# A delta-rule inverse from blocks of 16, with rows spread over partitions through DRAM instead of by products

## The chip, the cores and the metric

The kernel runs on one core of a Trainium2 chip. The metric is the device time of one execution in microseconds, as the median of several runs. Before the change it is 1660.73 us (three runs, 1659.98 to 1662.09).

The core has five engines that matter here, each working through its own list of instructions in order and waiting on semaphores for the others: TensorE (matrix products; PE in the profile, with the load of its weights as PEld), VectorE (DVE), ScalarE (ACT), GpSimd (POOL) and SyncE (SP), which only issues DMAs. TensorE writes its products into PSUM; everything else lives in SBUF, which has 128 partitions.

## What is computed

The reference is one step of a decoder layer over 256 prompt tokens and 32 sample tokens (8 sequences of 4). Cut to what matters:

```python
proj = x @ w_in                                   # 2048 -> 11280 columns
y_a  = (gB * conv3(gC * h)) @ w_a_out             # short gated convolution
q, k, v = split(silu(conv4(qkv)))                 # then the gated delta rule, 8 heads of 128
gcum  = cumsum(g)  within chunks of 64
decay = exp(gcum_i - gcum_j)  for i >= j
M = strict_lower(kb @ k.T * decay)
T = inverse(I + M)                                # 64 x 64, unit lower triangular, per chunk and head
u = T @ (v * beta);  w = T @ (kb * exp(gcum))
# scan over the 4 chunks with a state S (128 x 128 per head), then norm and gate
y_b = o @ w_b_out
x = LN(ALPHA * x + (sig(m_a) * y_a + sig(m_b) * y_b) @ w_o)
x = LN(ALPHA * x + relu(x @ w_up)**2 @ w_down)
```

All of it is float32. The inverse T and the decay are what the change touches.

## The kernel before

**Weight blocks.** The bulk is x @ W for six weight matrices, cut into 496 blocks of 512 KB each. `load` (line 177) brings a block in on SP's queue into one of four buffers `raw`; `split_hi` (line 187) rounds it on ScalarE into a high half `hi`; `split_lo` (lines 189 to 194, seen at line 142 because all VectorE products, sums and differences go through the helper `tt`) subtracts to get the low half `lo`; `matmuls` (lines 219 and 221) multiplies: 24 products per block, high with high, high with low, low with high. High and low halves have four buffers each, and both splits are issued three blocks ahead of their use (`AHEAD`). A weight load can go out when the low half of the block four before it is made, since that frees the buffer.

**Steps.** The main loop (lines 1644 to 1735) issues one step per block. In each, in this order: the high half three blocks ahead; one portion of the side work, up to the next `yield` of a generator; the low half three blocks ahead; what is due of the evacuations of finished column groups; the block's 24 products; the weight load seven blocks ahead. The order is written by hand. Nothing is rescheduled, so the side work's instructions stand on each engine between those of the weight stream, at the step where their `yield` puts them.

**Evacuations.** Blocks 0 to 47 give k, q and v of the two groups of four heads. Each group of four blocks is followed by a convolution of four taps per half: copies on ScalarE, three VectorE instructions over 312 columns each (line 145), and then a SiLU on ScalarE (lines 291 to 298).

**Side work.** `side` runs `gates`, then `gdn(0)`, then `gdn(1)`, one for each group of four heads. `gates` (line 1017) computes g and its sums in chunks. `gdn` (line 1122) goes through the delta rule. Its parts around the change are:

- Decay: the elements of g are multiplied with a triangular mask into `gl` (128 x 512), split into two rounded halves `glx`, and multiplied with a matrix of ones per chunk (line 1214), which gives every partition the running sums along a row. From this the exponent `E` is made.
- `nM`, the negative of M, stands with a 64-row chunk on each half of the partitions; eight such matrices lie side by side.
- Inverse of the diagonal blocks of 8: they are gathered into `n8` (line 1269), spread into `X` (512 wide), split into two rounded halves `mx`, and multiplied with a matrix of ones per block of 8 (line 1333), so that each partition holds all rows of its own block. Seven forward-substitution steps on VectorE (lines 1339 and 1340) give the inverse `u8`, one product and one sum over the eight matrices at a time.
- Joining blocks: the loop over s = 8, 16 (line 1356) joins neighbouring blocks, with two sets of small 32 x 32 products in each round (`pairs`, line 1328), a copy on ScalarE, and a predicated copy and a transpose on VectorE. A last round joins 32 to 64.
- Then the state products, the scan over the chunks, and the sample tokens.

`gdn(1)` begins only when `gdn(0)` has ended, and all side work has to end before the block `mark["merge"]` = 112, where the pool of its tiles is given up.

Of the kernel before, what the change touches and what calls it, by code (L numbers as in the profile page):

```python
# [9 lines left out]
F32 = mybir.dt.float32  # L10
F32R = mybir.dt.float32r
# [29 lines left out]
def _constants():  # L41
# [7 lines left out]
    f["hm"] = k // 64 == m // 64  # L49
    i = np.arange(64)[None, :]  # L50
    f["lc"] = (k % 64) <= i
    f["mbias"] = np.where((k % 64) <= i, 0.0, -1e30)
    f["mask8"] = (k % 64) // 8 == i // 8
    f["m8"] = (k % 32) // 8 == i[:, 0:32] // 8
    f["i8"] = k % 8 == np.arange(8)[None, :]
    f["i8u"] = k % 8 < np.arange(8)[None, :]
    f["bo8"] = k // 8 == m // 8
# [20 lines left out]
    early = ("hm", "bo8", "lcum", "lrem", "lcums", "lrems", "lsp", "bm3", "hmask")  # L78
# [11 lines left out]
    for s in (8, 16):  # L90
        g[s] = (j // (2 * s) == i // (2 * s)) & ((j // s) % 2 == 0) & ((i // s) % 2 == 1)
# [14 lines left out]
def hybrid_kernel(ctx: ExitStack, tc: tile.TileContext, A):  # L106
# [3 lines left out]
    def pool(name, bufs=1, **kw):  # L110
        return ctx.enter_context(tc.tile_pool(name=name, bufs=bufs, **kw))
# [6 lines left out]
    gp = pool("gp", 4, space=PSUM)  # L118

# [21 lines left out]
    def tt(out, a, b, op):  # L141
        dve.tensor_tensor(out=out, in0=a, in1=b, op=op)  # L142
# [114 lines left out]
    hmr, bo8 = (cp.tile([P, P], F32R, name=n) for n in ("hmr", "bo8"))  # L257
# [759 lines left out]
    def gates(first):  # L1017
# [17 lines left out]
        for t, n in ((hmr, "hm"), (bo8, "bo8")):  # L1035
            act.copy(t, cst(n))
# [30 lines left out]
        tt(gm, bmid(g[:, 2, :], 8), bc(cst("bm3"), 8), MUL)  # L1067
        sb = cp.tile([P, 2, 8], F32, name="gsb")
# [13 lines left out]
        pe.matmul(q[:, 136:144], cst("lrems"), g[:, 2, :], start=True, stop=True)  # L1082
        ge = cp.tile([P, 96], F32, name="gexp")
# [38 lines left out]
    def gdn(G):  # L1122
# [26 lines left out]
        gl = T([P, 4, 2, 64], "gl")  # L1149
# [38 lines left out]
        for n in range(4):  # L1188
# [7 lines left out]
        tt(gl, bc(G_["g"][:, :, pr], 64),  # L1196
           cst("lc").unsqueeze(1).unsqueeze(1).to_broadcast([P, 4, 2, 64]), MUL)
# [3 lines left out]
        glf = gl.rearrange("p c r x -> p (c r x)")  # L1201
        glx = pl.tile([P, 2, 512], F32R, tag="vml", name=nm("glx"))
# [9 lines left out]
        gr = gtile()  # L1212
        for u in range(2):
            pe.matmul(gr, hmr, glx[:, u], start=(u == 0), stop=(u == 1))
# [12 lines left out]
        tt(E, gr.rearrange("p (c r x) -> p c r x", c=4, r=2), bc(G_["ngc"][:, :, pr], 64), ADD)  # L1227
# [35 lines left out]
        n8 = sqr[:, 0:64].rearrange("p (q j) -> p q j", q=8)  # L1263
        u8 = sqr[:, 64:128].rearrange("p (q j) -> p q j", q=8)
        t8 = sqr[:, 128:192].rearrange("p (q j) -> p q j", q=8)
        i8 = cst("i8")
        tt(Tm, nM, bmid(cst("mask8"), 8), MUL)
        yield
        dve.tensor_reduce(out=n8, in_=Tm.rearrange("p q (b j) -> p q j b", b=8), axis=mybir.AxisListType.X, op=ADD)
        tt(n8, n8, bmid(cst("i8u"), 8), MUL)  # L1270
        tt(n8, n8, bmid(i8, 8), ADD)
        tt(X.rearrange("p q (k j) -> p q k j", k=8), n8.unsqueeze(2).to_broadcast([P, 8, 8, 8]),
           i8.unsqueeze(1).unsqueeze(3).to_broadcast([P, 8, 8, 8]), MUL)
        move_sums(1)
        yield
        Xf = X.rearrange("p q c -> p (q c)")
        mx = pl.tile([P, 2, 512], F32R, tag="vml", name=nm("mx"))
        act.copy(mx[:, 0], Xf)
# [11 lines left out]
        tt(mx[:, 1], Xf, mx[:, 0], SUB)  # L1290
# [40 lines left out]
        n88 = gtile()  # L1331
        for u in range(2):
            pe.matmul(n88, bo8, mx[:, u], start=(u == 0), stop=(u == 1))
        nb = n88.rearrange("p (q k j) -> p q k j", q=8, k=8)
        dve.tensor_copy(u8, bmid(i8, 8))
        for j in range(1, 8):
            if j == 5 or j == 3 and G == 0:
                yield
            tt(t8[:, :, 0:j + 1], u8[:, :, 0:j + 1], nb[:, :, 0:j + 1, j], MUL)
            dve.tensor_reduce(out=u8[:, :, j], in_=t8[:, :, 0:j + 1], axis=mybir.AxisListType.X, op=ADD)  # L1340
        tt(U.rearrange("p q (b j) -> p q b j", b=4), u8.unsqueeze(2).to_broadcast([P, 8, 4, 8]),
           cst("m8").rearrange("p (b j) -> p b j", b=4).unsqueeze(1).to_broadcast([P, 8, 4, 8]), MUL)
# [13 lines left out]
        for s in (8, 16):  # L1356
            px = gtile()
            pairs(px, lambda r, q, w: nM[r, q, 32 * (w % 2):32 * (w % 2) + 32], Tc)
            act.copy(Xc, px[:, 0:256].rearrange("p (q c) -> p q c", q=8))
            if s == 16:  # L1360
                move_v(1)
            yield
            pq = gtile()
            pairs(pq, lambda r, q, w: Xc[r, q, :], U)
            dve.copy_predicated(U, bmid(msk(s), 8), pq[:, 0:256].rearrange("p (q c) -> p q c", q=8))
            dve.transpose(out=Tf, in_=Uf)
            if s == 16:
                states_of(0)
            move_v(0 if s == 8 else 2)
            yield  # L1370
# [398 lines left out]
```

## Time and profile before

| | before |
|---|---|
| median of three runs | 1660.73 us (1659.98 to 1662.09) |
| span of the profiled execution | 1656.8 us |
| the profiled execution's own time | not listed apart from its span |
| TensorE busy | 1648.6 us, 13130 products |
| VectorE busy | 981.2 us, 1299 instructions |
| ScalarE busy | 785.8 us, 1231 instructions |
| GpSimd busy | 138.8 us, 273 instructions |
| DMA | 280.42 MB, 169 GB/s on average |

The profile shows one execution. The span goes from its first to its last instruction. A timeline row gives the start from the span's begin, the time, the engine, the line of the kernel, the operation, the tile written and those read, the shape and the number of instructions merged; in brackets stands the idle time before it and what ended it. A product in float32 is issued as two instructions, so 32 products show as x64. Products overlap: the pitch between starts, not the length, is what one takes from TensorE. In the list of DMAs a row has the number, the size and the median time from issue to landing.

### The profile page before, as it was taken

How to read it: one execution, taken by the hardware profiler on the slowest of the kernel's cores; microseconds unless marked ns; L12 is line 12 of the kernel's file. 1: busy time of each engine (PE TensorE's matmuls, PEld its weight loads, DVE VectorE, ACT ScalarE, POOL GpSimd, SP SyncE). 2: the span in 40 equal slices, each digit the busy share in tenths (PEclk: the TensorE clock that was granted, in tenths of full speed). 3: DMA queues.
4: the chain of work that ended last, by engine and by line, in shares of the span. 5: the costliest groups of instructions: out<-in, count | busy, mean ns of one | idle time of the engine just before them, and what ended most of it. 6: DMA issues, size and time to landing. Idle time of an engine off the chain costs nothing.

```text
span 1656.8 us, 31402 instructions
## 1 busy us (share of the span) xinstructions
PE 1648.6 (100%) x13130; PEld 1634.0 (99%) x13130; DVE 981.2 (59%) x1299; ACT 785.8 (47%) x1231; POOL 138.8 (8%) x273
## 2 busy tenths in 40 slices
PE   9999999999999999999999999999999999999998
PEld 8999999999999999999999999999999999999997
DVE  6798678767544444457776666444444444444466
ACT  6786756448533333334444455443334433344354
POOL 1142216133000000000000000000000000000011
PEclk9999999999999999999999999999999999999999
DMA  8555457545555555554565555555555555555552
GB/s 272 176 169 172 135 173 203 184 130 175 185 170 165 166 165 165 166 166 157 167 217 164 166 166 166 166 166 166 165 166 166 166 166 165 166 166 166 180 162 100
DMA packets 273236, 280.42 MB, mean 169 GB/s; under 512 B 13727, under 2 KB 267220, under 8 KB 272832
## 3 DMA queue, kind: packets, MB, share of 16 engines
q1 hardware_dynamic: 269334, 266.33, 51.2%
q0 software_dynamic: 3616, 12.02, 2.6%
q8 instruction: 103, 1.69, 0.4%
q14 instruction: 39, 0.32, 0.1%
q10 hardware_dynamic: 144, 0.07, 0.0%
HBM read 270.88 MB, written 7.48 MB: 168 GB/s over the span
## 4 chain that ended last, share of the span: by engine, by line
PE 98%; DVE 1%; ACT 1%; DMA 0%; issue 0%; SPq 0%; ACTq 0%
PE acc L219 62%; PE acc L221 31%; PE acc L739 1%; PE g L1328 0%; PE g L1500 0%; PE g L1520 0%; PE g L1523 0%; DMA xr<-in_x_prompt_dram 0%; PE g L1319 0%; PE g L1220 0%; PE g L1478 0%; DVE lo L142 0%; PE g L1512 0%; DVE w L145 0%; DVE Y L145 0%
## 5 line engine op out<-in xcount | busy, mean ns | idle before, releaser
L142 DVE TENSOR_TENSOR lo<-raw,hi 128x1024 fp32r<-128x1024 f32 (+1 forms) x503 | 607.3, 1210 | 576.7 <-ACT hi L187 573.7
L187 ACT CAST hi<-raw 128x1024 fp32r<-128x1024 f32 (+1 forms) x499 | 519.1, 1043 | 729.5 <-PE acc L219 657.0
L219 PE MATMUL acc<-xh,hi 128*128 128x288 f32 x1408 | 397.9, 298 | 0.3 <-ACT xh L946 0.2
L219 PE MATMUL acc<-xl,hi 128*128 128x288 f32 x1408 | 394.2, 295 | 0.0
L221 PE MATMUL acc<-xh,lo 128*128 128x288 f32 x1408 | 302.6, 296 | 0.2 <-DVE lo L142 0.2
L219 PE MATMUL acc<-dl,hi 128*128 128x288 f32 (+1 forms) x1024 | 287.7, 295 | 0.0
L219 PE MATMUL acc<-dh,hi 128*128 128x288 f32 (+1 forms) x1024 | 287.4, 295 | 0.0
L219 PE MATMUL acc<-hl,hi 128*128 128x288 f32 x992 | 277.8, 295 | 0.0
L219 PE MATMUL acc<-hh,hi 128*128 128x288 f32 x992 | 277.4, 294 | 0.0
L219 PEld LDWEIGHTS acc<-xh,hi 128*128 128x128 f32 x1408 | 264.4, 188 | 3.1 <-issue 1.6
L219 PEld LDWEIGHTS acc<-xl,hi 128*128 128x128 f32 x1408 | 264.2, 188 | 1.1 <-DVE xl L142 0.3
L221 PEld LDWEIGHTS acc<-xh,lo 128*128 128x128 f32 x1408 | 226.0, 188 | 0.7 <-DVE lo L142 0.6
L221 PE MATMUL acc<-dh,lo 128*128 128x288 f32 (+1 forms) x1024 | 219.8, 296 | 0.0
L221 PE MATMUL acc<-hh,lo 128*128 128x288 f32 x992 | 213.2, 296 | 0.0
L219 PEld LDWEIGHTS acc<-dh,hi 128*128 128x128 f32 x1024 | 193.3, 189 | 0.0
L219 PEld LDWEIGHTS acc<-dl,hi 128*128 128x128 f32 x1024 | 192.8, 188 | 0.0
L219 PEld LDWEIGHTS acc<-hh,hi 128*128 128x128 f32 x992 | 186.4, 188 | 0.4 <-issue 0.4
L219 PEld LDWEIGHTS acc<-hl,hi 128*128 128x128 f32 x992 | 186.1, 188 | 0.0
L221 PEld LDWEIGHTS acc<-dh,lo 128*128 128x128 f32 x1024 | 164.5, 188 | 0.0
L221 PEld LDWEIGHTS acc<-hh,lo 128*128 128x128 f32 x992 | 159.0, 188 | 0.0
L219 PE MATMUL acc<-mh,hi 128*128 128x288 f32 x256 | 71.9, 297 | 0.0
L219 PE MATMUL acc<-ml,hi 128*128 128x288 f32 x256 | 71.7, 295 | 0.0
(423 smaller groups left out, 1489.1 us busy)
## 6 DMA issues: line engine op xcount, KB each, us to landing
raw<-in_w_in_dram SPq DMA_DIRECT2D x175, 512.0 KB, 3.5
raw<-in_w_up_dram SPq DMA_DIRECT2D x128, 512.0 KB, 3.6
raw<-in_w_down_dram SPq DMA_DIRECT2D x128, 512.0 KB, 3.6
raw<-in_w_o_dram SPq DMA_DIRECT2D x32, 512.0 KB, 3.7
raw<-in_w_a_out_dram SPq DMA_DIRECT2D x16, 512.0 KB, 3.6
raw<-in_w_b_out_dram SPq DMA_DIRECT2D x16, 512.0 KB, 3.6
S<-in_state_gdn_dram POOLq DMA_DIRECT2D x8, 512.0 KB, 5.5
out_dram<-S POOLq DMA_DIRECT2D x8, 512.0 KB, 4.7
```

What stands on the lines that cost most here:

```text
L142: dve.tensor_tensor(out=out, in0=a, in1=b, op=op)
L187: act.copy(his[i][:, k:k + step], raw[i][:, k:k + step])
L219: pe.matmul(o, h[:, k, c], x, start=st and x is xh_, stop=False)
L221: pe.matmul(o, l[:, k, c], xh_, start=False, stop=en)
L739: pe.matmul(out, x[:, kk, c], w[:, k, :], start=False, stop=stop)
```

## The change

Two things are replaced.

*The gates' sums.* In `gates`, two POOL copies regroup g into `by_row`, and two products of it with the triangular matrix give the running sums of all heads with a row of tokens on one partition. ScalarE copies them out, and SP stores them to DRAM (`sums_d`). In `gdn`, one SP load reads the group's sums back, repeated over 64 partitions each, into `gl`. The masked product, the split and the spreading product go away.

*The inverse.* The diagonal blocks are now 16 wide. They are gathered into `n16`, stored to DRAM by SP (all columns as `low_d`, the right half, which ScalarE first copies into `n8`, as `high_d`), and loaded back one step later, repeated over the 16 partitions of each block: rows 0 to 7 into `low` (128 x 1024), rows 8 to 15 into `high` (128 x 512). Substitution runs over the first 8 columns, then one 512-wide product and a reduction apply those to the right half, then substitution runs over the last 8. The round s = 8 with its small products, its copy, its predicated copy and its transpose goes away. The number of `yield`s changes: from the gathering to the first set of small products the first group takes four blocks more than before, and everything from the second round on comes two blocks later, in the second group likewise.

Constants that are no longer used (`hm`, `bo8`, `lc`, `mask8` and others) are dropped from the table that is loaded at the start.

```diff
+        by_row = cp.tile([P, 16], F32, name="by_row")
+        for r in range(2):
+            gps.tensor_copy(by_row[:, 8 * r:8 * r + 8].rearrange("p (n a b) -> p n a b", n=2, a=2),
+                            g[:, 0:2, :].rearrange("p b (n r a) -> p r n a b", n=2, r=2)[:, r])
...
+        for r in range(2):
+            pe.matmul(q[0:8, 144 + P * r:144 + P * r + P], by_row[:, 8 * r:8 * r + 8], cst("lcum"),
+                      start=True, stop=True)
+        gq = cp.tile([8, 256], F32, name="gq")
+        act.copy(gq.rearrange("p (s r x) -> p s r x", s=2, r=2),
+                 q[0:8, 144:400].rearrange("p (r s x) -> p s r x", r=2, s=2))
+        sp.dma_start(sums_d.rearrange("n b x -> (n b) x"), gq)
...
-        tt(gl, bc(G_["g"][:, :, pr], 64),
-           cst("lc").unsqueeze(1).unsqueeze(1).to_broadcast([P, 4, 2, 64]), MUL)
+        sp.dma_start(gl, sums_d[2 * G:2 * G + 2].rearrange("n b x -> n (b x)").unsqueeze(1).to_broadcast([2, 64, 512]))
...
-        act.copy(glx[:, 0], glf)
-        tt(glx[:, 1], glf, glx[:, 0], SUB)
-        for u in range(2):
-            pe.matmul(gr, hmr, glx[:, u], start=(u == 0), stop=(u == 1))
...
+        tt(Tm, nM, bmid(cst("mask16"), 8), MUL)
+        yield
+        dve.tensor_reduce(out=n16, in_=Tm.rearrange("p q (b j) -> p q j b", b=4), axis=mybir.AxisListType.X, op=ADD)
+        tt(n16, n16, bmid(cst("i16u"), 8), MUL)
+        tt(n16, n16, bmid(i16, 8), ADD)
+        act.copy(n8, n16[:, :, 8:16])
+        sp.dma_start(low_d[G].rearrange("b k x -> (b k) x"), sqr[:, 0:P])
+        sp.dma_start(high_d[G].rearrange("b k x -> (b k) x"), sqr[:, 384:448])
         move_sums(1)
         yield
-        mx = pl.tile([P, 2, 512], F32R, tag="vml", name=nm("mx"))
-        act.copy(mx[:, 0], Xf)
+        for t, d, k in ((low, low_d[G], 0), (high, high_d[G], 8)):
+            t_src = d[:, k:k + 8].rearrange("b k x -> b (k x)")
+            sp.dma_start(t, t_src.unsqueeze(1).to_broadcast([8, 16, t_src.shape[1]]))
...
-        for u in range(2):
-            pe.matmul(n88, bo8, mx[:, u], start=(u == 0), stop=(u == 1))
+        def substitute(u, n):
+            for j in range(1, 8):
+                tt(t16[:, :, 0:j + 1], u[:, :, 0:j + 1], n[:, :, 0:j + 1, j], MUL)
+                dve.tensor_reduce(out=u[:, :, j], in_=t16[:, :, 0:j + 1], axis=mybir.AxisListType.X, op=ADD)
+                if j == 5 or j == 3 and G == 0:
+                    yield
+        dve.tensor_copy(u16, bmid(i16, 8))
+        yield from substitute(u16, low)
+        tt(lows, u16[:, :, 0:8].unsqueeze(2).to_broadcast([P, 8, 8, 8]),
+           low[:, :, :, 8:16].rearrange("p q k j -> p q j k"), MUL)
+        dve.tensor_reduce(out=t16[:, :, 0:8], in_=lows, axis=mybir.AxisListType.X, op=ADD)
+        tt(u16[:, :, 8:16], u16[:, :, 8:16], t16[:, :, 0:8], ADD)
+        yield
+        yield from substitute(u16[:, :, 8:16], high)
...
-        for s in (8, 16):
-            px = gtile()
-            pairs(px, lambda r, q, w: nM[r, q, 32 * (w % 2):32 * (w % 2) + 32], Tc)
...
+        move_v(0)
+        if G == 0:
+            yield
+        px = gtile()
+        pairs(px, lambda r, q, w: nM[r, q, 32 * (w % 2):32 * (w % 2) + 32], Tc)
```

More of the change, by code (lines that the diff above doesn't have):

```diff
@@ L118, in hybrid_kernel @@
     gp = pool("gp", 4, space=PSUM)
+    dp = pool("dp", space=bass.MemoryType.DRAM)
     counter = [0]
@@ L256, in hybrid_kernel @@
     epsc = cp.tile([P, 3], F32, name="epsc")
-    hmr, bo8 = (cp.tile([P, P], F32R, name=n) for n in ("hmr", "bo8"))
+    hmr = cp.tile([P, P], F32R, name="hmr")
+    sums_d = dp.tile([4, 2, 256], F32, name="sums_d")
+    low_d = [dp.tile([8, 16, P], F32, name=f"low_d{G}") for G in range(2)]
+    high_d = [dp.tile([8, 16, 64], F32, name=f"high_d{G}") for G in range(2)]
     stBA = cp.tile([P, 32, 32], F32, name="stBA")
@@ L1034, in gates @@
         yield
-        for t, n in ((hmr, "hm"), (bo8, "bo8")):
-            act.copy(t, cst(n))
         ba = gd["pool"].tile([P, 2, NT], F32, tag="hs", name="ba")[:, 0, :]
@@ L1148, in gdn @@
         states_in(1)
-        gl = T([P, 4, 2, 64], "gl")
+        gl = T([P, 512], "gl")
         ss = T([P, 18], "ss")
```

72 lines of the change are left out of this document (25 added, 47 removed).

## The prediction

> **What bounds the kernel now.** I read the page's busy shares and the chain that ended last first, then the granted clock, then the timelines of TensorE, VectorE and ScalarE around the delta rule of the first head group.
>
> ```profile
> span 1656.8 us, 31402 instructions
> PE 1648.6 (100%) x13130; PEld 1634.0 (99%) x13130; DVE 981.2 (59%) x1299; ACT 785.8 (47%) x1231; POOL 138.8 (8%) x273
> PE 98%; DVE 1%; ACT 1%; DMA 0%; issue 0%; SPq 0%; ACTq 0%
> core 0: 1656.8 us, clock 0.999
> ```
>
> TensorE is busy all the way, is 98% of the chain, and its clock is not throttled (0.999). So time taken off its stream comes off the span, unless something that feeds it becomes late. The span is 1656.8; the median of the runs is 1660.73, so 3.9 us lie around the span. I make the sum on the span and carry it over to the median.
>
> **What the removed products cost.** The timeline of TensorE prices them. Columns are start, length, engine, line, operation.
>
> ```profile
> 138.00 0.43 PE L221 MATMUL acc<-xh,lo 128*128 128x288 f32 x2
> ...
> 138.40 0.30 PE L219 MATMUL acc<-xl,hi 128*128 128x288 f32 x1
> ...
> 138.81 0.43 PE L221 MATMUL acc<-xh,lo 128*128 128x288 f32 x2
> 139.16 0.75 PE L1328 MATMUL g<-U,gl 32*32 32x32 f32 x64
> ...
> 140.08 0.30 PE L219 MATMUL acc<-xl,hi 128*128 128x288 f32 x1
> ...
> 142.87 0.43 PE L221 MATMUL acc<-xh,lo 128*128 128x288 f32 x2
> ...
> 144.15 0.30 PE L219 MATMUL acc<-xl,hi 128*128 128x288 f32 x1
> ```
>
> With nothing in between, the second L219 starts 0.40 after the L221 row (138.00 to 138.40). With the first set of small products (line 1328) between, it is 1.27 (138.81 to 140.08): they cost 0.87. The second set, a block later, comes between 142.87 and 144.15: 1.28, so 0.88. The change drops the round s = 8, one set of each in both head groups: 2 x 1.75 = 3.50.
>
> ```profile
> 122.18 0.29 PE L219 MATMUL acc<-xh,hi 128*128 128x288 f32 x1
> ...
> 122.58 0.29 PE L219 MATMUL acc<-xl,hi 128*128 128x288 f32 x1
> 123.09 0.53 PE L221 MATMUL acc<-xh,lo 128*128 128x288 f32 x2 [0.22 <-DVE lo L142]
> 123.47 0.30 PE L219 MATMUL acc<-xh,hi 128*128 128x288 f32 x1
> ...
> 125.59 0.43 PE L221 MATMUL acc<-xh,lo 128*128 128x288 f32 x2
> 125.86 0.62 PE L1333 MATMUL g<-mx,bo 128*128 128x512 f32 x2
> ...
> 126.45 0.29 PE L219 MATMUL acc<-xl,hi 128*128 128x288 f32 x1
> ```
>
> The spreading product L1333 costs (126.45 - 125.59) - 0.40 = 0.46, in both groups 0.92. Between its rows stands the only visible stall of this stretch: L221 at 123.09, 0.51 after its predecessor instead of 0.13, and the next row 0.38 later instead of 0.27. That is 0.49 us of waiting for VectorE's low half of block 33, which starts at 122.18.
>
> ```profile
> 74.31 0.31 PE L1081 MATMUL g<-be,ao 128*128 128x8 f32 x2
> ...
> 74.70 0.38 PE L219 MATMUL acc<-xh,hi 128*128 128x288 f32 x1
> ...
> 94.04 0.72 PE L1214 MATMUL g<-glx,hmr 128*128 128x512 f32 x2
> 94.69 1.97 PE L1220 MATMUL g<-kq 128*64 128x128 f32 x32
> ```
>
> The gates' product L1214 goes too. It holds the queue from 94.04 to 94.69, 0.65, of which about 0.15 is the turn-over after the transposes that stay: 0.50, in both groups 1.00. Added are two products of 8 weights by 128 columns: between 0.12 (1.97 us over the 16 products of L1220, each in two passes) and 0.20 (L1081 and L1082 take the 0.39 from 74.31 to 74.70). I take 0.16, between the two: the weights are as few as L1220's are many, the depth the same. That adds 0.32 (0.24 to 0.40). TensorE's own work: 3.50 + 0.92 + 1.00 - 0.32 = 5.10 us less.
>
> **What the change does to the feeders.** A block's high half (ScalarE) and low half (VectorE) are made three blocks ahead. VectorE is in order, so side work ahead of a split delays it.
>
> ```profile
> 119.49 1.17 DVE L1269 TENSOR_REDUCE vmh<-xt 128x64 f32<-128x512 f32 x1
> 120.70 0.48 DVE L142 TENSOR_TENSOR vmh<-vmh,cf 128x64 f32<-128x64 f32 x2
> 121.21 0.69 DVE L142 TENSOR_TENSOR xt<-vmh,cf 128x512 f32<-128x512 f32 x1
> ...
> 126.28 1.70 DVE L145 SCALAR_TENSOR_TENSOR w<-w,hw 128x312 f32<-128x312 f32 x3
> 127.90 1.22 DVE L142 TENSOR_TENSOR lo<-raw,hi 128x1024 fp32r<-128x1024 f32 x1
> 129.03 1.69 DVE L145 SCALAR_TENSOR_TENSOR w<-w,hw 128x312 f32<-128x312 f32 x3
> ...
> 102.14 0.69 DVE L1239 TENSOR_REDUCE ss<-xt 128x8 f32<-128x512 f32 x1
> ...
> L1340 DVE TENSOR_REDUCE vmh<-vmh 128x8 f32<-128x16 f32 (+6 forms) x7 | 1.4, 198 | 0.2
> L142 DVE TENSOR_TENSOR vmh<-vmh,g 128x16 f32<-128x16 f32 (+6 forms) x7 | 1.4, 195 | 0.2
> ```
>
> Per group VectorE loses the 512-wide product that builds X (0.69), the two subtractions for the rounded copies (0.69 each), the gates' product (0.69), one predicated copy and one transpose of 256 (0.44 each, between the 0.24 of 64 elements and the 0.69 of 512): 3.64. It gains a second substitution of 14 instructions (7 x 0.198 + 7 x 0.195 and gaps, 2.9), one 512-wide product and one 512-wide reduction (0.69 each), one addition (0.22, a 64-wide one like those at 120.70), and 0.12 on the two 128-wide instructions: 4.6. One us more in total, but two of the savings (the gates' product and its subtraction) lie where VectorE was not pressed. ScalarE loses two constant copies and three casts, and gains the copies gq and n8; POOL gains two small gathers of the gates, three steps ahead of their use, at a time when it waits for the gates anyway: nothing.
>
> One added wait is not hidden. The copy n8 stands on ScalarE ahead of the SiLU of its step and waits for VectorE's 16-wide rows.
>
> ```profile
> 114.73 1.28 ACT L296 ACT_TABLE_LOAD   x1
> ...
> 119.61 0.42 ACT L296 ACTIVATE kq<-w 128x256 f32<-128x256 f32 x1 [3.04 <-DVE w L145]
> ...
> 120.06 1.03 ACT L187 CAST hi<-raw 128x1024 fp32r<-128x1024 f32 x1
> ```
>
> Now the table load and one SiLU pass while VectorE works, and the cast of block 34 starts at 120.06. Afterwards: the reduction starts at 119.49, the rows are ready 1.17 + 0.57 later at 121.25, the copy at 121.5, the table load at 122.8, two SiLU pairs (0.45 each) at 123.7, the cast ends at 124.75, the low half of block 34 at 126.0. TensorE, without the old stall and without L1333, starts block 34 at 122.18 + 3.19 = 125.37 and wants the low half 0.53 later, at 125.9. So the stall at block 33 goes (its low half comes 0.57 earlier) and one of about 0.1 (0 to 0.4) at block 34 comes.
>
> From there the first group runs close. VectorE by its own pitches (a low half 1.13, 127.90 to 129.03; a convolution 1.62, 126.28 to 127.90; a pair of substitution steps 0.40 to 0.50): low halves of blocks 35 and 36 at 127.2 and 130.0; the first substitution starts at 131.6; block 37 at 134.2, 38 at 136.2, 39 at 140.0, 40 at 143.9, 41 at 147.5, 42 at 150.5. TensorE, at 3.19 a block, wants block 41 at 148.3 and 42 at 151.5: 0.8 and 1.0 to spare, the least of all. After that the small products lengthen the blocks again. In the second group these four-tap convolutions are over, 6.5 us of VectorE in this stretch, and I allow it 4 to spare. I put 0.4 (0 to 0.9) for both new stalls, against 0.49 removed.
>
> Here a rule weighs against the change. The added 512-wide product and the substitution's operand are read with steps of 512 or 256 bytes. L1269, read with a step of 32 bytes, took 1.17 us; L1239, over as many elements in a row, 0.69: 0.92 ns more per element. The same on 512 + 2 x 280 elements would add 0.5 + 0.5, of which 0.95 lies ahead of block 41 and turns 0.8 to spare into 0.15 late. [...]
>
> **The DMAs.** Eleven are added, all on SP among the weight loads: one store of the gates' sums, and per group one load of them, two stores and two loads of the rows.
>
> ```profile
> raw<-in_w_in_dram SPq DMA_DIRECT2D x175, 512.0 KB, 3.5
> out_dram<-Y SPq DMA_DIRECT2D x8, 256.0 KB, 2.3
> out_dram<-S POOLq DMA_DIRECT2D x8, 512.0 KB, 4.7
> g<-in_ln_b_dram POOLq DMA_DIRECT2D x1, 1024.0 KB, 10.0
> ```
>
> On SP each weight load waits for the low half that frees its buffer. The stores wait for something earlier on VectorE and ScalarE than the weight load behind them, so they delay it by their issue alone. The loads of the rows are issued a step later and wait for the stores to land: 121.25 + 2.3 (4.7 at most) = 123.6 to 126, when SP would wait for block 34's low half (126.0) anyway. The row load of 512 KB then takes 3.5 (like a weight load) to 10.0 (the slower broadcast, twice as large, on POOL's queue): I take 5, nearest to the weight load on the same queue, so 129 to 131. VectorE wants it at 131.9. Both legs may take 10.6 us, and the rows give 5.8 to 14.7. The load of the sums has three blocks, 9.6 us. The 768 KB per group that push the next weight load back have 2 us and more at block 38. Cost: nothing; with the far ends, 14.7 - 10.6 - 0.8 = 3.3 us in the first group.
>
> Later steps of the side work move back by two blocks.
>
> ```profile
> 410.14 0.89 POOL L1487 DMA_DIRECT2D out_dram<-S  x1 [2.40 <-DVE S L145]
> ...
> 421.98 2.21 ACT L1705 CAST ahl<-ao 128x1152 fp32r<-128x1152 f32 x2 [1.52 <-issue]
> ```
>
> The last state store then falls near 410.1 + 6.4 = 416.5 and lands 4.7 later, 421.2, before ScalarE's cast behind the pool's end at 421.98, whose result is first used four blocks on: nothing.
>
> **The sum.** -5.10 - 0.49 + 0.4 = -5.2: span 1651.6, median 1655.5.
>
> **The rivals.**
> 1. VectorE becomes the bound in the first group: its new instructions cost 0.1 more each than the rows say. Nineteen of them lie ahead of block 41: 1.9 - 0.8 = 1.1 stalled; with a late row load of 3.3 at most, 4.4. It ends between 1656.5 and 1659.5, say 1658.5, within 0.2%. For it: VectorE's rows from 119.49 to 129.03 follow one another almost without idle time. Against it: the durations are measured on the same shapes.
> 2. The strided rule on top of the sum: 1655.8 with 0.3 more. [...]
> 3. Slower: the sixteen-fold reads of the same DRAM rows go one after another, so that the 512 KB take 16 us. The rows land at 139.6, 7.7 after they are wanted, and 6.9 reach TensorE in the first group; in the second 3.9 (8 late, 4 to spare): -5.2 + 10.8 gives 1666.3. It decides from about 13 us for that load (5.2 of stalls over both groups). Against it: the two rows of 1024 KB are each one row of DRAM read for 128 partitions, and the slower landed in 10.0.
> 4. The removal buys nothing because TensorE waits anyway: 1660.7. Against it: its only stall there is 0.49.
>
> **How the numbers follow.** Forecast 0.62, rival 2 0.10, rival 1 0.14, rival 3 0.10, rival 4 0.04. Faster by over 0.2% means under 1657.4 (0.2%, 3.3 us, is about what a measurement of this kernel tells from no change): the first two and a part of rival 1, 0.74. Within 0.2%: 0.16. Slower: 0.10. The likeliest case by itself spans 1655.0 (no new stall, cheap products) to 1656.5. The range adds 0.7 below for the spread of the medians and reaches up to rival 1: 1654.3 to 1660.0, leaving rival 3 and the edges out.
>
> **What would show it.** Right: one set of 64 small products before the state products instead of two, no L1333 or L1214; block 33 without a wait, a wait under 0.4 at block 34; the substitution's reduction no slower than 0.2; row loads landing in some 5 us. Wrong: idle TensorE with VectorE as releaser between blocks 36 and 42, VectorE waiting for the row load, or weight casts waiting for DMAs.

## The result: slower, and where the profile shows it

The changed kernel takes 1668.37 us (median of five runs, 1665.04 to 1670.26) against 1660.73 (five runs, 1659.98 to 1662.09): a ratio of 1.0047 with a 95% interval of 1.0035 to 1.0059. It is 7.6 us slower, where 5.2 us less were forecast. The profiled execution took 1669.76 us, its span is 1668.0.

The page of the changed kernel, with the lines that answer to those shown of the kernel before:

```profile
span 1668.0 us, 30920 instructions
...
PE 1651.2 (99%) x12870; PEld 1636.9 (98%) x12870; DVE 984.2 (59%) x1321; ACT 782.5 (47%) x1226; POOL 135.7 (8%) x275
...
PE 97%; DVE 2%; DMA 1%; ACT 0%; issue 0%; SPq 0%; ACTq 0%; DVEq 0%
...
raw<-in_w_in_dram SPq DMA_DIRECT2D x175, 512.0 KB, 4.1
```

TensorE has 260 instructions fewer, but shows more busy time (1651.2 after 1648.6): the products themselves have become slower somewhere. VectorE and the DMAs, 1% and 0% of the chain before, now have 2% and 1%. The list of TensorE's waits says where:

```profile
PE g L1332 <- DVE U L1353: 5.0, 1, 5.0
PE g L1332 <- ACT xt L1371: 3.3, 1, 3.3
...
PE acc L218 <- DVE lo L139: 0.7, 2, 0.5
```

Both long waits are at line 1332, the small products that join blocks of 16. One is in each head group. The same list of the kernel before has no wait of a small product. TensorE's timeline around them, first group and then second:

```profile
157.86 0.43 PE L218 MATMUL acc<-xh,lo 128*128 128x288 f32 x2
161.58 1.08 PE L1332 MATMUL g<-U,xt 32*32 32x32 f32 x64 [3.29 <-ACT xt L1371]
162.59 1.94 PE L1323 MATMUL g<-S,b 128*32 128x128 f32 x32
164.46 0.61 PE L216 MATMUL acc<-xh,hi 128*128 128x288 f32 x1
164.86 0.44 PE L216 MATMUL acc<-xl,hi 128*128 128x288 f32 x1
165.10 0.44 PE L216 MATMUL acc<-xh,hi 128*128 128x288 f32 x1
...
167.60 0.29 PE L216 MATMUL acc<-xl,hi 128*128 128x288 f32 x1
167.73 0.29 PE L216 MATMUL acc<-xh,hi 128*128 128x288 f32 x1
...
327.21 0.42 PE L218 MATMUL acc<-xh,lo 128*128 128x288 f32 x2
332.69 1.08 PE L1332 MATMUL g<-U,gl 32*32 32x32 f32 x64 [5.05 <-DVE U L1353]
333.70 0.61 PE L216 MATMUL acc<-xh,hi 128*128 128x288 f32 x1
334.10 0.44 PE L216 MATMUL acc<-xl,hi 128*128 128x288 f32 x1
...
338.27 0.29 PE L216 MATMUL acc<-xl,hi 128*128 128x288 f32 x1
...
339.03 0.75 PE L1332 MATMUL g<-U,xt 32*32 32x32 f32 x64
```

The weight products behind a small set stand in the same in-order queue, so the whole stream stops for 3.29 and 5.05 us although their operands are ready. And after each wait everything runs at half speed: the small set takes 1.08 instead of the 0.75 it takes at 339.03, the weight products start every 0.24 us instead of every 0.13, until 167.5 and 338.1. Stretches of the same trace with the granted clock (columns: the stretch, its length, busy time of TensorE, its weight load, VectorE, ScalarE and GpSimd; clock; DMA share; GB/s) give the cause:

```profile
158.00:162.00 4.00, 0.70 (x35) 0.47 (x37) 3.93 (x7) 3.69 (x11) 3.56 (x4) 0.82 0.31 94
162.00:164.40 2.40, 2.40 (x83) 1.91 (x72) 2.33 (x4) 2.27 (x6) 2.27 (x4) 0.50 0.66 215
...
168.00:172.00 4.00, 4.00 (x83) 3.60 (x82) 1.22 (x1) 2.84 (x6) 0.00 (x0) 1.00 0.28 96
...
332.60:338.20 5.60, 5.51 (x83) 5.45 (x84) 4.74 (x6) 2.63 (x6) 3.05 (x4) 0.51 0.53 172
```

In this trace the granted clock falls to 0.50 while TensorE is idle (at 160.57 and 331.24) and comes back at 167.40 and 338.06, after some microseconds of work. The last section has these stretches for more runs.

Why the small products wait is different in the two groups. In the first, U is ready, but the copy Xc (line 1371) stands on ScalarE behind a move of the values (line 1303), and that waits for VectorE's transpose of the values. VectorE's row and ScalarE's:

```profile
156.94 1.24 DVE L1361 STREAM_TRANSPOSE U<-vf 128x1024 f32<-128x1024 f32 x1
...
158.22 0.82 ACT L1303 COPY v<-U 32x256 f32<-32x256 f32 x2 [4.43 <-DVE U L1361]
...
160.22 1.04 ACT L184 CAST hi<-raw 128x1024 fp32r<-128x1024 f32 x1
161.17 0.36 ACT L1371 COPY xt<-g 128x256 f32<-128x256 f32 x1
```

The change itself put the move there. In the kernel before, ScalarE has the first copy Xc (line 1359) ahead of the first move (line 1299); there the move stood behind the set s = 8, and with that round gone it stands ahead of the only copy left:

```profile
139.96 0.37 ACT L1359 COPY xt<-g 128x256 f32<-128x256 f32 x1
...
144.02 0.81 ACT L1299 COPY v<-U 32x256 f32<-32x256 f32 x2
```

In the second group VectorE itself is late with U:

```profile
315.72 0.22 DVE L1342 COPY vmh<-cf 128x128 f32<-128x128 f32 x1
318.49 0.19 DVE L139 TENSOR_TENSOR vmh<-vmh,low 128x16 f32<-128x16 f32 x1 [2.56 <-DMA low<-low_d]
...
323.77 1.10 DVE L139 TENSOR_TENSOR xt<-vmh,low 128x512 f32<-128x512 f32 x1
...
332.19 0.45 DVE L1353 STREAM_TRANSPOSE U<-U 128x256 f32<-128x256 f32 x1
```

From the copy at 315.72 to the end of the transpose at 332.64 are 16.9 us: 2.56 of waiting for the row load, the two substitutions, the product between them, an evacuation and three low halves, almost without a gap. TensorE came to the small products at 327.6. The same rows of the kernel before, the last of them TensorE's:

```profile
303.62 0.19 DVE L1335 COPY vmh<-cf 128x64 f32<-128x64 f32 x1
...
308.61 0.45 DVE L1343 STREAM_TRANSPOSE U<-U 128x256 f32<-128x256 f32 x1
...
309.41 0.75 PE L1328 MATMUL g<-U,gl 32*32 32x32 f32 x64
```

There the way from the copy to the transpose's end took 5.4 us, and U was ready 0.35 before TensorE came, 5.8 after the copy. The change makes the way 11.5 longer and gives it 6.1 more (327.6 is 11.9 after the copy): 11.5 - 6.1 - 0.35 is the 5.05 of the wait.

The starts of TensorE's blocks (every 24th weight product) give the account by stage, in microseconds; the last column is the version e11 below. Before block 15 the profiles differ by up to 2.6 us (it starts between 60.84 and 63.42 in all of them), with the arrival of the first inputs, so the account begins there. From block 115 to the end all three take 1228.3 or 1228.4 us.

| blocks | before | changed | difference | e11 |
|---|---|---|---|---|
| 15 to 28: gates, first group's L1214 | 45.40 | 45.57 | +0.17 | 45.56 |
| 28 to 36: L1333, block 33 | 26.46 | 25.69 | -0.77 | 25.69 |
| 36 to 70: first group | 128.77 | 134.08 | +5.31 | 127.03 |
| 70 to 78: second group's L1214 | 28.26 | 27.80 | -0.46 | 27.80 |
| 78 to 115: second group | 138.76 | 143.94 | +5.18 | 137.02 |
| sum | 367.65 | 377.08 | +9.43 | 363.10 |

The +5.31 is 3.29 of waiting, 2.5 of slow clock (0.33 on the small set, 0.86 on L1323, which takes 1.94 instead of 1.08, 1.3 on block 43) and 1.2 of late low halves at blocks 40 and 41, less 1.75 for the round that is gone. The +5.18 is 5.05 of waiting and 2.3 of slow clock, less 1.75 and 0.46 (L1333). The sum is larger than the 7.6 us of the medians; each column is one execution, and stages of the same code differ between executions: the first group, left as it is in e3, e4, e6, e7, e8 and e13 below, takes 131.6 to 134.3 us in them, with half-clock stretches of different length and with or without the late low halves.

### The profile page after: what moved, and what is told of

Read it like the earlier page. It is cut to its first block, busy times and chain, and to the rows that moved or that the text cites. A ratio compares the mean times of both kernels' runs of the same rounds, so it can differ in the third digit from the quotient of the medians.

```text
span 1668.0 us, 30920 instructions
## 1 busy us (share of the span) xinstructions
PE 1651.2 (99%) x12870; PEld 1636.9 (98%) x12870; DVE 984.2 (59%) x1321; ACT 782.5 (47%) x1226; POOL 135.7 (8%) x275
## 4 chain that ended last, share of the span: by engine, by line
PE 97%; DVE 2%; DMA 1%; ACT 0%; issue 0%; SPq 0%; ACTq 0%; DVEq 0%
PE acc L216 62%; PE acc L218 31%; PE acc L739 1%; DVE lo L139 0%; DMA low<-low_d 0%; PE g L1510 0%; PE g L1530 0%; PE g L1533 0%; PE g L1323 0%; DMA xr<-in_x_prompt_dram 0%; DVE vmh L139 0%; PE g L1221 0%; PE g L1488 0%; PE g L1522 0%; DVE vmh L1338 0%
```

## The experiments

Ratios are against the kernel before, run beside each of them.

**e1: the gates' sums alone.** The kernel before with `by_row`, `sums_d` and the load of `gl`; the inverse stays.

> The gates' sums through DRAM as in the change, the inverse as in the kernel before (two rounds of small products from blocks of 8). My theory is that the loss comes from the new inverse alone: TensorE's small products stand at the head of its in-order queue and wait 3.3 us (group 1, for ScalarE's copy) and 5.05 us (group 2, for VectorE's transposed inverse). Then this kernel has none of these waits; it saves the product L1214 (0.47 in both groups, as the blocks of the changed kernel show) and pays 0.6 for the two products by_row: 1660.73 - 0.94 + 0.6 = 1660.4. Rival: the sums' way through DRAM (VectorE waits for that load in the changed kernel) is a part of the loss: 1662 or more, with a new wait of TensorE behind the pairs L1221.

1659.34 us, ratio 0.9994 (0.9985 to 1.0003): no difference that can be told. Blocks 15 to 115 take 367.65 us, as before: L1214's removal (0.47 in each group) is paid back by the products `by_row`, 0.61 instead of the 0.32 of the prediction, and by small shifts. By themselves the sums through DRAM cost nothing; the loss needs the new inverse.

**e2: the values' transpose behind Xc, first group.**

```diff
+        def turn_v():          # transpose of vf, kdec's product, sum, move_v(0)
...
+        if G:
+            turn_v()
+        else:
+            yield
         px = gtile()
         pairs(px, ...)
         act.copy(Xc, ...)
+        if G == 0:
+            turn_v()
         move_v(1)
```

> The changed kernel, with the 1024-wide transpose of the values, kdec's product and the first move of the values put behind the copy Xc, in the first head group alone. Theory: the second set of small products of group 1 waited 3.3 us because ScalarE's copy Xc stood behind a move that waited 4.4 us for VectorE's transpose; the move now stands behind Xc, so this wait goes, and with it the slow TensorE that follows it (some 2.5 us): 1668.4 - 5.8 = 1662.6. Rival A, the slow TensorE after a wait costs nothing of its own: 1668.4 - 3.3 = 1665.1. Rival B, VectorE has more work than TensorE leaves it time for, and the wait only moves to the next product that needs VectorE (the round after, or a block's low half): 1667 to 1668.4.

1664.27 us, 1.0027 (1.0016 to 1.0038). The wait of 3.3 is gone, and blocks 36 to 70 take 128.51 us, 5.6 less than in the changed kernel's profile, but 3.1 to 5.8 less than in all the profiles with that group unchanged (131.6 to 134.3). Against the changed kernel the ratio falls by 0.0020, 3.3 us (the medians by 4.1), nearer to rival A's 3.3 than to the theory's 5.8; that the slow clock costs time of its own is shown by e6, not by this run. A new wait of 1.0 shows at the third set (line 1393), where copy and transpose now stand behind the moved work. Rival B falls: only 1.0 of the wait has moved.

**e3: small products of the second group two blocks later.**

```diff
         yield
         if G == 0:
             yield
+        else:
+            yield
+            yield
```

and the sample's work starts two steps earlier beside it, with two `yield`s less in the scan and the last moves.

> The changed kernel, with the small products of the second head group put two blocks later than now; two blocks are taken out of the steps after them, so that the side work ends where it ended. Theory: in group 2 VectorE needs some 14 us from the first step of the substitution to the transposed inverse, and TensorE comes to the small products after 11.8; two blocks give 6.4 us, less two low halves of 1.2, so the wait of 5.05 goes, and the slow products behind it (2.2): 1668.4 - 7.3 = 1661.1, up to 1662 with the later steps closer together. Rival B, VectorE stays behind for good and the wait appears at a later product: 1667 to 1668.4.

1661.73 us, 1.0010 (1.0001 to 1.0019). The 5.05 are gone; 0.8 remain, at the second set. Blocks 78 to 115 take 137.92 us, 6.0 less, and the ratio falls by 0.0037, 6.1 us, near the theory. The product had only to stand later in the list.

**e5: both repairs.**

> The changed kernel with both repairs: in group 1 the values' transpose behind the copy Xc, in group 2 the small products two blocks later. Theory: the two waits are separate places in TensorE's queue, so what each repair gave adds up. Measured, they gave 4.1 and 6.6 us: 1668.4 - 10.7 = 1657.7 (1656.5 to 1659), under the kernel before. Rival, the two groups share a cause (VectorE, which stays behind from the first to the second): less than the sum, 1660 or more.

1657.14 us, 0.9981 (0.9973 to 0.9990): faster than the kernel before. Blocks 15 to 115 take 365.81 us, 1.84 less than before and 11.3 less than in the changed kernel, where e2 gains 5.6 in its group and e3 6.0 in its own: nearly the sum, so the two waits are separate. Two short waits of the same kind are left:

```profile
PE g L1396 <- DVE U L1387: 1.0, 1, 1.0
...
PE g L1332 <- ACT xt L1379: 0.8, 1, 0.8
```

**e4, e7, e8: what makes U late in the second group.**

> The changed kernel, but the second group's spread rows are read from the first group's store (so the second group's inverses are those of wrong rows), and their loads are issued one step earlier, before the row sums; all instructions and transfers remain. It takes away VectorE's wait of 2.6 us for the row load in group 2 and leaves VectorE's work. Theory, VectorE's work and the late rows each are a part of the 5.05: the wait falls to 2.5 us, median 1668.4 - 2.6 = 1665.8; if the weight loads behind the rows are then what VectorE waits for, only to 4.3, 1667.6. Rival, the row load alone is the cause: no wait of the small products in group 2 and 1668.4 - 7.3 = 1661.1.

> The changed kernel, but in group 2 only an eighth of the spread rows is loaded (96 instead of 768 KB; the rest is set to zero by GpSimd, so group 2's inverses are wrong); VectorE's instructions are all there. Theory, both the traffic and VectorE's work are in the 5.05 us: VectorE doesn't wait for the rows (2.6 us), ScalarE's casts don't wait for weights (6.8 us now), and the small products wait 2.5 us, behind VectorE's work alone: 1668.4 - 2.6 = 1665.8, up to one us less if the slow stretch behind a shorter wait is shorter too. Rival A, VectorE's work alone is the cause: 5 us of wait and 1668.4. Rival B, the traffic alone: no wait, 1661.1.

> The changed kernel, but in group 2 the 14 instructions of the second substitution are left out, their steps kept (group 2's inverses are wrong); the rows are loaded as in the change. They take 2.9 us on VectorE. Theory: the small products' wait in group 2 falls from 5.05 to 2.1 us, median 1668.4 - 2.9 = 1665.5, up to one us less with a shorter slow stretch. Rival A, the late transfers alone set the wait: 5 us and 1668.4. Rival B, what is added on VectorE has no cover at all: the wait is gone only when the other added instructions go too, and what is saved is 2.9 in any case, as in the theory; the two differ in that here the low halves of the next blocks would come late too (waits of TensorE behind them).

e4 came out outside all its figures: 1669.37 us, 1.0057 (1.0044 to 1.0071), with a longer wait in the trace (the time cannot be told from the changed kernel's). Its side case had the cause, weight loads behind the rows, but not the size. ScalarE, VectorE and TensorE in it:

```profile
317.99 1.05 ACT L184 CAST hi<-raw 128x1024 fp32r<-128x1024 f32 x1 [5.64 <-DMA raw<-in_w_in_dram]
...
319.08 1.23 DVE L139 TENSOR_TENSOR lo<-raw,hi 128x1024 fp32r<-128x1024 f32 x1 [4.36 <-ACT hi L184]
...
334.66 1.08 PE L1339 MATMUL g<-U,gl 32*32 32x32 f32 x64 [7.75 <-DVE U L1360]
```

The rows came in time, and a weight load behind them came late instead: VectorE waited 4.36 for a low half ahead of the substitution instead of 2.56 for the rows. Moving one transfer forward made another late; what they share, no run shows. e7 takes most of the rows' transfer away and leaves VectorE's work; e8 does the opposite. TensorE's row in e7, then in e8:

```profile
328.19 1.07 PE L1336 MATMUL g<-U,gl 32*32 32x32 f32 x64 [3.48 <-DVE U L1357]
```

```profile
326.11 0.75 PE L1332 MATMUL g<-U,gl 32*32 32x32 f32 x64 [1.39 <-DVE U L1354]
```

With an eighth of the rows 3.48 us are left, with one substitution less 1.39; the ratios are 1.0031 (1.0019 to 1.0043) and 1.0016 (1.0007 to 1.0025). The casts' waits for weights in the whole run fall from 21.7 to 9.1 us in e7. So, by single traces, about 1.6 of the 5.05 are traffic and 3.7 VectorE's second substitution; neither alone is the cause. e7 left 1 us more than its theory had, because VectorE came to the substitution 0.9 us later in the stream (1.87 behind the start of block 84 instead of 0.99): it had waited 7.4 instead of 5.9 us for the load of the gates' sums. From the copy to the transpose's end e7 saves 2.45, about what the theory had. In e8 the clock did not fall after the 1.39 us, and the low halves of the second group came in time, so its rival B falls too.

**e6: products that keep TensorE busy.**

```diff
+        if G:
+            wq = gtile()
+            for n in range(38):
+                pe.matmul(wq[:, 0:NT], xh[:, n % KT, 0:P], xh[:, n % KT, 0:NT], start=True, stop=True)
         px = gtile()
```

> The changed kernel; in group 2, 38 products of 128 weights by 288 columns that nobody reads stand in TensorE's queue ahead of the small products that wait. At 0.133 us each they fill the 5.05 us of the wait and end when VectorE's transposed inverse is there. Theory: the 2.2 us behind the wait (products at 0.24 instead of 0.133 us, small products 1.08 instead of 0.75) are the price of the idle time, so with a busy TensorE they go, though the small products come no earlier: 1668.4 - 2.2 = 1666.2, small products at 0.75. Rival, the slow products have another cause (their operands, the traffic of that moment): no gain, 1668.4 or some more.

1664.43 us, 1.0032 (1.0019 to 1.0044), 0.0015 or 2.5 us less than the changed kernel; the two intervals overlap, so the trace has to carry this.

```profile
324.28 5.26 PE L1372 MATMUL g<-xh 128*128 128x288 f32 x38
329.64 0.75 PE L1332 MATMUL g<-U,gl 32*32 32x32 f32 x64
```

The small products start no earlier behind the block before them, but take 0.75, and the following block takes 5.07 us instead of 7.03. Blocks 78 to 115 take 2.13 less than in the changed kernel, as the theory had (2.2). The slow stretch is the price of the idleness; neither the operands nor the traffic of that moment make it.

**e9 to e12: towards a version without waits.** e9 puts the values' transpose and moves behind the masked copy in both groups, and gives kdec's product and the copy `n8` to GpSimd; e10 gives four low halves to GpSimd, too.

```diff
-        act.copy(n8, n16[:, :, 8:16])
+        gps.tensor_copy(n8, n16[:, :, 8:16])
...
+        gps.tensor_tensor(out=kdf, in0=kdf, in1=bc(qc(kdr), P), op=MUL)
...
+            if i - AHEAD in (37, 39, 84, 86):                     # e10
+                return gps.tensor_tensor(out=los[i], in0=r, in1=his[i], op=SUB)
```

> Built on the kernel with both repairs (1657.1). In both groups the values' transpose and their moves now stand behind the round's masked copy and transpose on VectorE and behind Xc on ScalarE; kdec's product (1.18 us on VectorE) and the copy n8 go to GpSimd. Theory: what is left of the loss are short waits of the same kind, by the trace of the kernel with both repairs 1.0 us (group 1, third set of small products behind VectorE's transpose), 0.8 (group 2, second set behind Xc) and 0.2 (block 34, behind n8): 1657.1 - 2.0 = 1655.1. Rival, the values come too late now: the moves (6.6 us on GpSimd) begin one or two blocks later, VectorE's scaling of v waits for them, and the first product with U128 with it: 1657 or more.

> The kernel before this one in the list, with four of the low halves (blocks 40, 42, 87 and 89, two in the stretch of each substitution) made by GpSimd instead of VectorE. Theory: VectorE has too much work in these two stretches; in the kernel with both repairs TensorE waits for low halves by 0.9 at block 41, 0.3 at 88 and 0.4 to 0.9 at 89; 1.2 us less for VectorE twice in each stretch takes these away: 1.5 to 2 us less than the kernel before it in the list, 1653.4. Rival, GpSimd takes more than the 6 us that these four blocks have, or slows VectorE down beside it: waits at blocks 40, 42, 87 or 89, and no gain.

e9: 1664.09 us, 1.0024 (1.0015 to 1.0033). No small product waits any more, but TensorE waits for low halves:

```profile
PE acc L218 <- DVE lo L139: 5.1, 6, 1.6
```

Neither of its cases names the cause, which lies in the copy `n8`. SP's, GpSimd's and VectorE's rows, first of e9 and then of e5:

```profile
306.93 1.77 POOL L1139 DMA_DIRECT2D S<-in_state_gdn_dram  x2
...
307.27 0.61 SPq L1281 DMA_DIRECT2D low<-low_d  x1
...
318.63 0.18 DVE L139 TENSOR_TENSOR vmh<-vmh,low 128x16 f32<-128x16 f32 x1 [5.83 <-DMA low<-low_d]
```

```profile
295.93 0.88 POOL L1139 DMA_DIRECT2D S<-in_state_gdn_dram  x1
...
306.12 0.60 SPq L1281 DMA_DIRECT2D low<-low_d  x1
...
313.22 0.19 DVE L139 TENSOR_TENSOR vmh<-vmh,low 128x16 f32<-128x16 f32 x1 [2.54 <-DMA low<-low_d]
```

GpSimd, now waiting for `n16` before its copy, issues two state loads of 512 KB 0.3 us before the row load instead of 10 us and more before it, and the rows land 11.4 us after their issue instead of 7.1. e11, which differs in the copy alone, confirms the copy as the cause; that the state loads are the link is read off these rows.

e10: 1669.37 us, 1.0050 (1.0038 to 1.0063), its rival. GpSimd takes 2.4 to 2.7 us for a low half, and VectorE is slowed beside it, for which rows stand further down; a cast waits 10.2 us for a weight load as well. Which of these makes most of the 5 us against e9 was not separated.

> The kernel with the later values' transpose and kdec's product on GpSimd, but the copy n8 back on ScalarE. In that kernel TensorE waited for no small product any more (all 1.0 and 0.8 us gone), but 5.1 us for low halves: the copy took 1.10 us on GpSimd instead of 0.24, the states' loads behind it on GpSimd were issued together with the row load instead of before it, which then landed 11.4 us after its issue instead of 7.1, and VectorE waited 7.9 us for rows instead of 2.5. Theory: with the copy back on ScalarE the rows land as in the kernel with both repairs, the low halves are on time but for some 2 us, and the gain of the order stands: 5 us under the kernel before, 1655. Rival, the order itself makes the low halves late (VectorE's transpose of the values one block later in a full queue): no better than the kernel with both repairs, 2.7 us under the kernel before or less.

> The one before in the list, and the loads of two of the four states per group (2 x 512 KB in each group) moved from GpSimd's queue, ahead of the row loads, to SP's queue behind the first substitution, some 10 us later and still four steps ahead of their use. Theory: the row load and the weight loads share the DMA engines with them; with them out of the way VectorE's wait for the rows of group 2 (2.5 us) shrinks to under 1, and the low halves that are late there (0.3 to 0.9 at the blocks 88 and 89) come in time: 0.5 to 1.2 us less than the one before. Rival, the rows wait for the weight loads alone, or the states now delay the weight loads behind them on SP: no gain, or up to 1 us more.

e11: 1656.84 us, 0.9982 (0.9973 to 0.9991). All waits of small products are gone; TensorE's small sets, here of the first group, run at full speed where the stream comes to them:

```profile
153.88 0.75 PE L1332 MATMUL g<-U,gl 32*32 32x32 f32 x64
157.95 0.75 PE L1332 MATMUL g<-U,xt 32*32 32x32 f32 x64
...
163.03 0.69 PE L1387 MATMUL g<-U,gl 32*32 32x32 f32 x32
```

Blocks 15 to 115 take 363.10 us, 4.55 less than before. In the medians it is 3.0 less (1.5 to 4.5), nearer to its rival (2.7) than to its theory (5) and not to be told from e5; the start-up of this profile was the latest of all. e12 (1656.61 us, 0.9981, 0.9972 to 0.9990) makes no difference to that: VectorE's wait for the rows falls from 2.6 to 1.6, and 0.6 comes back at Xc. Its rival holds.

**e13, e14: does the shape of the repeated read matter?** The rows are stored twice, so that the read goes over 16 (block and copy) instead of 8.

```diff
-            t_src = d[:, k:k + 8].rearrange("b k x -> b (k x)")
-            sp.dma_start(t, t_src.unsqueeze(1).to_broadcast([8, 16, t_src.shape[1]]))
+            t_src = d[:, :, k:k + 8].rearrange("b c k x -> (b c) (k x)")
+            sp.dma_start(t, t_src.unsqueeze(1).to_broadcast([16, 8, t_src.shape[1]]))
```

> The changed kernel, with the rows stored twice in DRAM, so that the repeated read has an outer dimension of 16 (block and copy) instead of 8; each partition still gets 4 KB and 2 KB. Theory, the read with 8 runs on fewer DMA engines: with 16 the row load of group 2 lands 4 to 5 us after its issue instead of 6.9, VectorE's wait for it falls from 2.6 to under 1, and the small products' wait from 5.05 to 3.5 to 4.5 us (3.5 is what VectorE's work leaves by itself): 1667 or, against the kernel before, 1.0035 to 1.0042 instead of 1.0047. Rival, the rows share the engines with the weight loads, and the outer dimension doesn't matter: 6.9 us or more, the two additional stores make it 0.5 later, and 1.0047 to 1.0052.

> The same in the version without waits of the small products (the values' transpose later, kdec's product on GpSimd, the copy n8 on ScalarE; 0.9982 of the kernel before). Theory: VectorE's wait for the rows of group 2 (2.6 us) falls to under 1, block 89's low half comes in time, 0.5 to 0.9 us less: 0.9977. Rival, no change in landing: 0.9982, or 0.3 us more for the stores on SP.

e13: 1667.23 us, 1.0045 (1.0031 to 1.0059). The rows land 6.7 us after their issue (309.46 to 316.2) instead of 6.9, and the small products wait 5.2. VectorE waits 1.6 for them instead of 2.56, but it came 1.1 us later in the stream itself. Going from 8 to 16 does not make the rows faster, though the casts wait less for weights (14.3 us instead of 21.7). The load of the gates' sums, whose outer dimension is 2, took 12.7 us for 256 KB in the second group of the changed kernel; no run gave that one another shape. e14: 1654.41 us, 0.9969 (0.9958 to 0.9981), the fastest kernel here, 5.1 us under the one before. But its interval overlaps e11's, and its blocks 15 to 115 take 362.98 us, as e11's 363.10: in the two profiles the difference lies before block 15 (61.15 and 63.42) and can't be put down to the rows. Why a repeated read of 512 KB lands later (6.7 to 6.9 us in e13 and the changed kernel) than a weight load of that size (4.1 in the median) stays open.

## Why the prediction was wrong

Point by point, by its own steps:

- **TensorE's own work, 5.10 us less: right but for one term.** The two products `by_row` cost 0.61, above the range of 0.24 to 0.40, and L1214 gave 0.47 each instead of 0.50, so the block times of the changed kernel give about 4.75 (3.50 + 0.93 + 0.93 - 0.61). In e11, where no small product waits, blocks 15 to 115 are 4.55 us shorter; that holds the 0.49 of block 33's stall, too, and e11's other order.
- **Block 33's stall goes, a small one comes at block 34: right.** The blocks 28 to 36 are 0.77 shorter, and block 34 takes 0.19 longer than a plain one (0.1 was forecast, 0 to 0.4).
- **"From there the first group runs close": the size was off.** Block 41 was given 0.8 to spare; the low halves of 40 and 41 came late by 1.2 together, outside the 0 to 0.9 allowed for both new stalls. In e8 and e13, with the same first group, they came in time, so this part changes with the execution.
- **The step that failed is the feeders' part as a whole: it looked at low halves alone.** The small products, too, stand in TensorE's queue and are fed by VectorE (U) and by ScalarE (Xc). When these are ready was never worked out, nor how that moves against the blocks that the change adds ahead of the first set. In the first group the diff itself shows `move_v(0)` ahead of the copy Xc, and TensorE waited 3.29 us. In the second, "I allow it 4 to spare" was made from convolutions and for low halves; the kernel before has 0.35 to spare for U (309.06 to 309.41), and U came 5.05 us late. With both waits taken out (e5) the loss is gone.
- **"The DMAs. Cost: nothing": wrong.** The rows took 6.9 us to land instead of 5, and 11.4 from the rows' being ready, so VectorE waited 2.56; the weights behind them came late. e7 puts this at 1.6 to 2.5 of the 5.05. The load of the sums, given 9.6, took 12.7 in the second group (issued at 276.79, used at 289.53), and VectorE waited 5.91 for it. In e1 this makes U 0.55 later in the second group and costs a wait of 0.18; in the changed kernel no run separates its part of the 5.05.
- **Not in the prediction: what the clock does behind a wait.** Behind the two waits 2.5 and 2.3 us were lost at half clock.
- **"3.9 us lie around the span": a misreading.** In all later runs the time is 1.7 to 2.2 us above the span (1669.76 and 1668.0 here), so the profiled execution of the kernel before was some 2 us faster than the median. No term of the sum hangs on it, but the spans differ by 11.2 where the medians differ by 7.6.
- **The strided rule (rival 2): the first half held.** The 512-wide product took 1.10 us instead of 0.69, close to the 0.5 priced for it; the substitution's 14 products from `low` took 0.19 to 0.27, at most 0.05 more each.
- **Rival 3 had the sign and not the mechanism:** its 16 us were the author's assumption, on no row; the row load took 6.9 us, not the 13 and more from which it would decide.
- **What would show it wrong** was named in part: VectorE waiting for the rows and casts waiting for weights came. Between blocks 36 and 42 VectorE released TensorE only for the late low halves (0.7 us idle); the 3.29 at block 42 ended with ScalarE, and the 5.05 with VectorE lies at block 88. The order of the side work's end, two blocks later, cost nothing, as forecast.

## What to carry to other kernels

Where one engine's queue is in order, each side instruction in it is a due time for all its feeders, not only the main stream's operands: for every product that a change moves or whose inputs it lengthens, work out when its operand is ready and when the queue comes to it. The 0.35 us that U had to spare stood in the trace of the kernel before. The repair is then cheap: two steps later in the list in one group, and a copy ahead of an unrelated move in the other, turned +7.6 us into -2.7 (e5). The waits of 3.29 and 5.05 us cost 1.8 and 1.5 times themselves, with the 2.5 and 2.3 us lost at half clock behind them.

## What the runs showed of the hardware

**TensorE's clock after a wait.** Waits of 3.0 to 7.7 us were followed by a stretch at half clock, and the one of 1.39 us (e8) by none. The traces hold when the granted clock changed:

| run, group | wait | half clock, from and to | us |
|---|---|---|---|
| changed, first | 3.29 | 160.57, 167.40 | 6.83 |
| changed, second | 5.05 | 331.24, 338.06 | 6.82 |
| e6, first | 3.3 | 159.34, 162.75 | 3.41 |
| e7, first | 3.3 | 159.40, 162.81 | 3.41 |
| e8, first | 3.03 | 160.91, 164.33 | 3.42 |
| e4, second | 7.75 | 330.28, 340.52 | 10.24 |

So in these runs the stretch lasted one, two or three steps of 3.41 us, and a wait of 3.3 us cost one step (e6, e7) or two (the changed kernel). In the changed kernel's trace all changes lie on one grid of that step (160.57 and 331.24 are 50 steps apart), and from execution to execution the grid lies differently against the work: the fall came 2.28 us after the start of the first group's wait in the changed kernel, 3.09 in e6 and 4.30 in e8. In e8 the small set, which came 3.03 after that start, still ran at 0.75, and the clock fell 1.3 us after it began. Laid over TensorE's rows, the steps that ended in a fall held 2.28 and 3.41 us of idle TensorE in the changed kernel, 2.14 in e8 and, the least between blocks 15 and 115 in the sixteen traces, 1.85 in e10; no step at full clock with up to 1.61 (e9) was followed by a fall. What sets the step, and what lets the clock fall, no run shows.

**VectorE beside GpSimd in e10.** Rows of both:

```profile
146.99 2.39 POOL L191 TENSOR_TENSOR lo<-raw,hi 128x1024 fp32r<-128x1024 f32 x1 [15.11 <-ACT hi L184]
...
147.73 1.74 DVE L139 TENSOR_TENSOR vmh<-vmh 128x64 f32<-128x64 f32 x1
```

The addition of 64 elements takes 0.22 in the changed kernel; beside GpSimd's instruction it took 1.74 and ended only when that did (149.47 and 149.38). The reduction ahead of it, with one operand, kept its 0.69 (147.01) beside the same instruction. A product of 56 elements took 2.46 beside a low half of 2.69, and 0.26 without one (144.78). So work given to GpSimd was not free for VectorE here: these two instructions took 1.5 and 2.2 us more. What holds them up, no run shows.
